# Two feed-forward up-projections in fp16 halves: weight sums move to VectorE, the norm scale moves into the norm weights, one accumulator pair takes turns over three PSUM banks

## The chip, the cores and the metric

The kernel runs on one core of one Trainium2 chip. A core has TensorE (matrix products into PSUM, eight banks of 128x512 fp32), VectorE, ScalarE and GpSimd (element-wise work, the last without PSUM), and SyncE, whose queue issues nearly all transfers between HBM and SBUF. Each engine works through its own queue in order and waits on semaphores. The metric is the device time of one execution in microseconds.

## What is computed

The reference is one layer of a transformer: half a SwiGLU feed-forward block, a token mixer with two kinds of attention, and half a SwiGLU block again, each behind an RMS norm; 1024 tokens, model width 1024, hidden width 2816. The change lies in the two feed-forward blocks:

```python
def rmsnorm(x, g):
    xf = x.astype(jnp.float32)
    y = xf * lax.rsqrt(jnp.mean(xf * xf, axis=-1, keepdims=True) + EPS)
    return (y * g.astype(jnp.float32)).astype(x.dtype)

def swiglu(h, w1, w3, w2):
    return (jax.nn.silu(h @ w1) * (h @ w3)) @ w2

h = rmsnorm(x, ffn1_norm[l])
x = x + 0.5 * swiglu(h, ffn1_w1[l], ffn1_w3[l], ffn1_w2[l])
```

All of it is fp32. TensorE multiplies in narrower formats, so the kernel splits an operand into a hi and a lo part and adds three products (hi by hi, hi by lo, lo by hi).

## The kernel before

**Work and layout.** Activations lie transposed, features on the 128 partitions (eight tiles k) and tokens along the row, in two halves tb of 512. A block runs in two stages: `ffn_up` (L309) computes silu(h w1) * (h w3) for 22 blocks of 128 hidden columns and stores them to HBM, and `ffn_down` (L522) multiplies by w2. Between the two blocks lies the token mixer, which the change does not touch.

**The up-projection.** The first four column blocks (pairs 0 and 1) are multiplied plainly in fp32 halves (L357 to L372), the accumulators being the PSUM banks X, Y and Z, two of each. Meanwhile `scale_h` (L237) forms the normed activations: x times gain times R (the reciprocal root of the mean square). `right_sums` (L274) forms four differences of them. Both leave fp16 halves by `split16` (L93): ScalarE rounds to fp16 with a scale (L94), VectorE computes what is left (L95). The scale is a power of two per norm, `K.hs`, found once in `gain_scales` (L115); its inverse is `K.hinv`.

The remaining 18 column blocks run as nine pairs fp = 2 to 10 (L412), each as one 2x2 block product with seven multiplications in place of eight (Winograd's form). The left operand has four raw blocks of 128x1024 in fp32, a11, a21, a22 and a12, loaded a pair ahead (`load`, L330). From them come four sums (L425 to L428): s1 = a21 + a22, a21 = a11 - a21, a11 = s1 - a11, s4 = a12 - a11. In pair 2 VectorE forms them, in the later pairs GpSimd (L424). `form` (L317) splits each operand into fp16 halves w: ScalarE makes hi (L94), VectorE lo (L95). The scale of a pair, a power of two, comes from the sums of squares of its raw blocks: ScalarE squares (L340), a small matmul `tot` (L344) adds over partitions, and VectorE derives `sc` and its inverse `si` (`find_scale`, L342; `pow2_scale`, L98).

TensorE's products of a pair stand, in the program's text, in this order; each is 24 matmuls of L397, twelve into each of two banks m:

| product | bank | weights, activations | read afterwards by |
|---|---|---|---|
| first product | X | a11, B11 | ScalarE, as sv (L407) |
| ws2 | Y | a11 (as a sum), T[1] | VectorE, u2 (L433) |
| ws1 | Z | s1, T[0] | |
| wa12 | X, added on | a12, B21 | ScalarE and VectorE, c11 (L442, L443) |
| ws3 | Y, added on | a21 (as a difference), T[2] | VectorE, u3 (L433, with Z L455) |
| wa22 | Y, added on | a22, T[3] | VectorE, c21 (L433) |
| ws4 | Z, added on | s4, B22 | VectorE, u2 (L469) |

Y is thus written three times in a pair and read after each; a product that is added on can start in a bank when the read before it is done, and the ws2 product of the next pair when c21 has been read. The first product of the next pair stands ahead of wa22 in the text.

Behind a product, `finish_a` (L507) applies silu on ScalarE and a product on GpSimd, and `act_sums` (L476) forms four differences on GpSimd and stores them (saT). `left_sums` (L493) loads two blocks of w2, forms four sums of them on VectorE (L503) and stores them (sw); eleven such jobs and two of `plain_sums` are spread over the pairs.

**What sets the order.** The text names dependences; a scheduler that estimates times decides the order in which each engine's instructions stand. A change of one engine's work therefore moves others too. Buffers are few: `po`, `sums` and `ex` have one of each name, so an add into u2 waits for the store of the pair before, and a w2 load for the store of the sums before.

Of the kernel before, what the change touches and what calls it, by code (L numbers as in the profile page):

```python
# [7 lines left out]
F32 = mybir.dt.float32  # L8
# [5 lines left out]
ALU = mybir.AluOpType  # L14
# [77 lines left out]

def split16(nc, t, src, scale):  # L93
    nc.scalar.activation(out=t[:, 0], in_=src, func=AF.Copy, scale=scale)  # L94
    return nc.vector.scalar_tensor_tensor(out=t[:, 1], in0=src, scalar=scale, in1=t[:, 0], op0=ALU.mult, op1=ALU.subtract)  # L95

# [18 lines left out]
def gain_scales(K, pool):  # L115
    nc = K.nc
    sq = pool.tile([P, 4, KD], F32, tag="gsq", name="gsq")
    nc.vector.tensor_tensor(out=sq, in0=K.gain, in1=K.gain, op=ALU.mult)
    r = pool.tile([P, 4], F32, tag="gr", name="gr")
    nc.vector.tensor_reduce(out=r, in_=sq, axis=AX.X, op=ALU.add)  # L120
    tot = K.pt.tile([P, TB], F32, tag="acc", name="tot")[:, 0:4]
    nc.tensor.matmul(tot, lhsT=K.ones, rhs=r, start=True, stop=True)
    K.hs, K.hinv = pow2_scale(K, pool, tot, 57)

# [112 lines left out]
def scale_h(K, tb, gi, gates=None):  # L237
    nc = K.nc
    K.h[tb], last = [None] * KD, []
    hs = K.hs[:, gi:gi + 1]  # L240
    for k in [i // 2 + i % 2 * (KD // 2) for i in range(KD)] if gates else range(KD):
        x = K.x[tb][k]
        g = K.gain[:, gi, k:k + 1]
        if gates:
            order_after(K, nc.scalar.activation(out=x, in_=x, func=AF.Copy, scale=g), gates[k])
            nc.gpsimd.tensor_tensor(out=x, in0=x, in1=K.R[tb], op=ALU.mult)
        else:
            nc.vector.scalar_tensor_tensor(out=x, in0=x, scalar=g, in1=K.R[tb], op0=ALU.mult, op1=ALU.mult)
        if gates:
            K.h[0][k] = K.hp.tile([P, 2, TB], F16, tag=f"hi0_{k}", name="h16")  # L250
            split16(nc, K.h[0][k], x, hs)
            continue
        hi = K.hp.tile([P, TB], F32R, tag=f"hi{tb}_{k}", name="hi")
        lo = K.hp.tile([P, TB], F32R, tag=f"lo{tb}_{k}", name="lo")
        last.append(split(nc, hi, lo, x))
        K.h[tb][k] = hi, lo
    if gates:
        K.b22 = []
        for k in range(KD // 2):
            K.b22.append(K.hp.tile([P, 2, TB], F16, tag=f"lo0_{k}", name="h16"))  # L260
            split16(nc, K.b22[k], K.x[1][k + KD // 2], hs)
    return last
# [10 lines left out]

def right_sums(K, tp, gi):  # L274
    nc = K.nc
    h = KD // 2
    T = [[], [], [], []]

    def put(i, k, src):
        t = (tp if i else K.hp).tile([P, 2, TB], F16, tag=f"t{i}_{k}" if i else f"lo0_{k + h}", name="tf")  # L280
        split16(nc, t, src, K.hs[:, gi:gi + 1])
        T[i].append(t)
    for k in range(h):
        b11, b21, b12, b22 = K.x[0][k], K.x[0][k + h], K.x[1][k], K.x[1][k + h]
# [24 lines left out]
def ffn_up(K, w13, w2, ctx0, gi, first):  # L309
# [7 lines left out]
    def form(src, sc):  # L317
        n = len(K.wpools)
        t = K.wpools[K.nw % n].tile([P, 2, KD, P], F16, tag=("whi", "wlo")[K.nw // n % 2], name="w16")
        K.nw += 1  # L320
        split16(nc, t.rearrange("p a k c -> p a (k c)"), src.rearrange("p k c -> p (k c)"), sc)
        return t
# [26 lines left out]
    with ExitStack() as c1:  # L349
# [7 lines left out]
        for tb, p in ((0, 0), (0, 1), (1, 1), (1, 0)):  # L357
            for f in range(2):
# [10 lines left out]
                else:  # L369
                    nc.scalar.activation(out=t, in_=u[0], func=AF.Silu)  # L370
                nc.vector.tensor_tensor(out=t, in0=u[1], in1=t, op=ALU.mult)
                store(2 * p + f, tb, t)  # L372
# [7 lines left out]
    K.nw = 0  # L380
    T = right_sums(K, open_pool(K, ctx, "tf", 1, side="right"), gi)
    ctx0.close()
    with ctx:
        pt = open_pool(K, ctx, "up_tot", 1, True)
        sums = open_pool(K, ctx, "up_sums", 1)
        rw.append(open_pool(K, ctx, "up_raw2", 1))
# [23 lines left out]
        n0, n1 = NPLAIN, NF // 2  # L410
        X, sv = first_product(r[0][0], scale, inv)
        for fp in range(n0, n1):  # L412
# [12 lines left out]
            se.tensor_tensor(out=s1, in0=a21, in1=a22, op=ALU.add)  # L425
# [1216 lines left out]
```

## Time and profile before

| | us |
|---|---|
| three runs | 2984.49, 2988.92, 2989.84; median 2988.92 |
| profiled execution | 2990.17, span 2988.4 |
| first block: plain pairs 0 and 1 / nine pairs | to 104.09 / 104.09 to 466.03 |
| first block, down-projection | from 466.03 |
| second block, nine pairs | 2403.20 to 2759.57 |
| TensorE, VectorE, ScalarE, GpSimd busy | 2835.6, 1995.5, 1370.2, 951.9 |
| mean granted TensorE clock | 0.986 of full speed |

In the views a row names line, engine, operation, output <- inputs; PE is TensorE, PEld its weight loads, DVE VectorE, ACT ScalarE, POOL GpSimd, SPq the transfer queue. A row of a timeline begins with start and length in us; what stands in brackets is the idle time of that engine in front of it and what ended it. A row of the groups ends with busy time, mean ns of one and idle time in front. Lines of code are those of the kernel before.

### The profile page before, as it was taken

To read this page: it belongs to the slowest core of one execution; us is meant where nothing else is said; L and a number is where in the kernel's file an instruction comes from. 1 tells how busy PE (TensorE), PEld (TensorE's weight loads), DVE (VectorE), ACT (ScalarE), POOL (GpSimd) and SP (SyncE) were. 2 spreads that over 40 slices of the span, in tenths; PEclk is the share of its full clock that TensorE was granted. 3 is DMA by queue.
4 is the path that set the end of the run, shared out by engine and by line. 5 is a ranking of instruction groups with operands and counts; after the bars stand their busy time and mean duration, and the time that the engine had idled before them with its cause. 6 is when DMAs were issued, how large, how long until landed. Compare 5 with 4: busy or idle time off the path is not lost. (4 is left out here: it accounts for less than half of the span.)

```text
span 2988.4 us, 40209 instructions
## 1 busy us (share of the span) xinstructions
PE 2835.6 (95%) x14276; PEld 2128.7 (71%) x14276; DVE 1995.5 (67%) x3282; ACT 1370.2 (46%) x2347; POOL 951.9 (32%) x765
## 2 busy tenths in 40 slices
PE   8998999999999899989899999999999998999998
PEld 6543447888788688778788888888878853444886
DVE  7866566666587467667777777776333966665656
ACT  7434334443333145445566666666432644432443
POOL 3348441000145123322333333333242436554101
PEclk9999999999999999999999999999999999999999
DMA  4354447655456544544332235222743246444854
GB/s 159 117 194 170 178 155 267 214 189 163 147 200 230 184 142 169 186 157 163 127 117 86 82 115 161 79 83 77 289 152 109 77 149 208 173 151 157 298 183 148
DMA packets 212712, 478.21 MB, mean 160 GB/s; under 512 B 20896, under 2 KB 39584, under 8 KB 212512
## 3 DMA queue, kind: packets, MB, share of 16 engines
q1 hardware_dynamic: 212512, 475.65, 46.2%
q8 instruction: 112, 1.84, 0.3%
q14 instruction: 88, 0.72, 0.1%
HBM read 313.56 MB, written 162.00 MB: 159 GB/s over the span
## 5 line engine op out<-in xcount | busy, mean ns | idle before, releaser
L397 PEld LDWEIGHTS <-w 128*128 128x128 f16 x3024 | 298.4, 99 | 414.4 <-issue 45.9
L52 PE MATMUL gm<-hi,whi 128*128 128x512 f32 x880 | 352.1, 400 | 3.3 <-ACT whi L89 1.9
L397 PE MATMUL Y<-tf,w 128*128 128x512 f16 x1296 | 304.2, 389 | 48.0 <-DVE u L433 29.0
L54 PE MATMUL gm<-hi,wlo 128*128 128x512 f32 x880 | 348.4, 397 | 0.3 <-DVE wlo L85 0.3
L53 PE MATMUL gm<-lo,whi 128*128 128x512 f32 x880 | 348.3, 396 | 0.0
L861 PE MATMUL S<-kt,qt 128*128 128x320 f32 (+5 forms) x1152 | 274.9, 352 | 36.4 <-ACT Pt L870 12.2
L85 DVE TENSOR_TENSOR tl<-tr,th 128x512 fp32r<-128x512 f32 (+2 forms) x384 | 236.2, 619 | 88.3 <-ACT th L89 85.0
L89 ACT ACTIVATE th<-tr 128x512 fp32r<-128x512 f32 (+2 forms) x384 | 203.8, 542 | 198.2 <-PE tr L916 194.7
L85 DVE TENSOR_TENSOR wlo<-st,whi 128x1024 fp32r<-128x1024 f32 x154 | 197.4, 1299 | 112.6 <-ACT whi L89 111.5
L868 DVE CUSTOM_DVE_ANT_0 S<-S,slab 128x896 f32<-128x896 f32 (+7 forms) x320 | 224.4, 708 | 65.5 <-PE S L861 59.5
L53 PE MATMUL acc<-wlo,whi 128*128 128x512 f32 (+1 forms) x628 | 243.1, 387 | 1.0 <-DVE wlo L85 1.0
L54 PE MATMUL acc<-whi,wlo 128*128 128x512 f32 (+1 forms) x628 | 242.1, 388 | 0.0
L89 ACT ACTIVATE whi<-st 128x1024 fp32r<-128x1024 f32 x154 | 160.6, 1057 | 177.2 <-PE acc L54 107.4
L52 PE MATMUL acc<-whi 128*128 128x512 f32 (+1 forms) x628 | 240.4, 387 | 0.0
L1027 POOL TENSOR_SCALAR Ps<-Ps,l 128x384 f32<-128x384 f32 (+7 forms) x128 | 100.8, 787 | 425.0 <-DVE l L1025 216.4
L861 PEld LDWEIGHTS S<-kt,qt 128*128 128x128 f32 x1152 | 183.4, 190 | 61.0 <-ACT Pt L870 14.2
L397 PE MATMUL X<-h,w 128*128 128x512 f16 x864 | 195.1, 379 | 0.0
L52 PEld LDWEIGHTS gm<-hi,whi 128*128 128x128 f32 x880 | 168.5, 191 | 36.3 <-ACT whi L89 2.1
L54 PEld LDWEIGHTS gm<-hi,wlo 128*128 128x128 f32 x880 | 168.1, 191 | 36.8 <-DVE wlo L85 0.9
L95 DVE SCALAR_TENSOR_TENSOR w<-a,sc,w 128x1024 f16<-128x1024 f32 x90 | 180.3, 2019 | 18.8 <-ACT w L94 17.4
L53 PEld LDWEIGHTS gm<-lo,whi 128*128 128x128 f32 x880 | 168.6, 192 | 30.8
L85 DVE TENSOR_TENSOR wlo<-wst,whi 128x1024 fp32r<-128x1024 f32 x103 | 137.0, 1332 | 44.1 <-ACT whi L89 32.9
(320 smaller groups left out, 6260.8 us busy)
## 6 DMA issues: line engine op xcount, KB each, us to landing
wst<-in_win_dram SPq DMA_DIRECT2D x55, 512.0 KB
sw<-w2s SPq DMA_DIRECT2D x44, 512.0 KB
st<-sw SPq DMA_DIRECT2D x88, 256.0 KB
st<-saT SPq DMA_DIRECT2D x88, 256.0 KB
a<-in_f1w_dram SPq DMA_DIRECT2D x36, 512.0 KB
a<-in_f2w_dram SPq DMA_DIRECT2D x36, 512.0 KB
st<-saB SPq DMA_DIRECT2D x66, 256.0 KB
qt<-sq SPq DMA_DIRECT2D x128, 128.0 KB
```

What stands on the lines that cost most here:

```text
L52: first = nc.tensor.matmul(out, lhsT=w[0][:, wk], rhs=x[0], start=start, stop=False, skip_group_check=skip)
L53: nc.tensor.matmul(out, lhsT=w[0][:, wk], rhs=x[1], start=False, stop=False, skip_group_check=skip)
L54: nc.tensor.matmul(out, lhsT=w[1][:, wk], rhs=x[0], start=False, stop=stop, skip_group_check=skip)
L85: return nc.vector.tensor_tensor(out=lo, in0=src, in1=hi.bitcast(F32), op=ALU.subtract)
L89: nc.scalar.activation(out=hi, in_=src, func=AF.Copy)
L95: return nc.vector.scalar_tensor_tensor(out=t[:, 1], in0=src, scalar=scale, in1=t[:, 0], op0=ALU.mult, op1=ALU.subtract)
L397: K.mark = nc.tensor.matmul(o, lhsT=w[:, a, m * h + k], rhs=x[k][:, b], start=start and k == 0 and i == 0, stop=k == h - 1 and i == 2, ski ...
L861: K.last = nc.tensor.matmul(S[:, o:o + n], lhsT=q, rhs=k[:, k0 + c:k0 + c + n], start=i == 0, stop=i == 1)
L868: nc.vector.tensor_tensor_reduce(out=sv, in0=sv, in1=mv, scale=-0.125, scalar=BIG, op0=ALU.add, op1=ALU.min, accum_out=nm)
L1027: nc.gpsimd.tensor_scalar(out=p[:, 0:n], in0=p[:, 0:n], scalar1=l[:, c:c + 1], scalar2=1.0, op0=ALU.mult, op1=ALU.mult)
```

## The change

Four edits. (1) The scale of the norm, `hs`, is multiplied into the norm weights once (`K.gs`); activations come out scaled, so `split16` copies and subtracts without a scale, and the plain products of the second token half are multiplied by `K.hinv` where they are read. (2) `form` keeps the weights' scale and holds the two instructions itself. (3) All weight sums are formed by VectorE. (4) Y takes two of three banks in turn, Y0, Y1 and a new Y2: pair 2 has Y0 and Y1, pair 3 has Y2 and Y0, pair 4 Y1 and Y2, and so on.

```diff
-def split16(nc, t, src, scale):
-    nc.scalar.activation(out=t[:, 0], in_=src, func=AF.Copy, scale=scale)
-    return nc.vector.scalar_tensor_tensor(out=t[:, 1], in0=src, scalar=scale, in1=t[:, 0], op0=ALU.mult, op1=ALU.subtract)
+def split16(nc, t, src):
+    nc.scalar.activation(out=t[:, 0], in_=src, func=AF.Copy)
+    return nc.vector.tensor_tensor(out=t[:, 1], in0=src, in1=t[:, 0], op=ALU.subtract)
...
-    K.hs, K.hinv = pow2_scale(K, pool, tot, 57)
+    hs, K.hinv = pow2_scale(K, pool, tot, 57)
+    K.gs = pool.tile([P, 4, KD], F32, tag="gs", name="gs")
+    nc.vector.tensor_tensor(out=K.gs, in0=K.gain, in1=hs.unsqueeze(2).broadcast_to([P, 4, KD]), op=ALU.mult)
...
-        g = K.gain[:, gi, k:k + 1]
+        g = K.gs[:, gi, k:k + 1]
...
-        split16(nc, t.rearrange("p a k c -> p a (k c)"), src.rearrange("p k c -> p (k c)"), sc)
+        hi, lo, src = [v.rearrange("p k c -> p (k c)") for v in (t[:, 0], t[:, 1], src)]
+        nc.scalar.activation(out=hi, in_=src, func=AF.Copy, scale=sc)
+        nc.vector.scalar_tensor_tensor(out=lo, in0=src, scalar=sc, in1=hi, op0=ALU.mult, op1=ALU.subtract)
...
-                    nc.scalar.activation(out=t, in_=u[0], func=AF.Silu)
-                nc.vector.tensor_tensor(out=t, in0=u[1], in1=t, op=ALU.mult)
+                    nc.scalar.activation(out=t, in_=u[0], func=AF.Silu, scale=K.hinv[:, gi:gi + 1])
+                if tb == 0:
+                    nc.vector.tensor_tensor(out=t, in0=u[1], in1=t, op=ALU.mult)
+                else:
+                    nc.vector.scalar_tensor_tensor(out=t, in0=u[1], scalar=K.hinv[:, gi:gi + 1], in1=t,
+                                                   op0=ALU.mult, op1=ALU.mult)
...
+        p3 = open_pool(K, ctx, "up_y", 1, True)
...
-            Y, Z = [[bank(n, m) for m in range(2)] for n in "YZ"]
-            se = nc.vector if fp == n0 else nc.gpsimd
+            Z = [bank("Z", m) for m in range(2)]
+            Y = [ps.tile([P, TB], F32, tag=f"Y{b}", name="Y") if b < 2 else p3.tile([P, TB], F32, tag="Y2", name="Y")
+                 for b in ((2 * (fp - n0) + m) % 3 for m in range(2))]
+            se = nc.vector
```

The scheduler's order differs from before only in the nine pairs of each block and just ahead of them; TensorE, ScalarE and SyncE issue the same instructions as before, GpSimd 64 fewer, VectorE 65 more. In the changed kernel `form`'s two halves are L323 and L324, the four sums L435 to L438, the matmuls of the pairs L405, the small matmul L347, the adds L443, L465 and L479.

VectorE at the end of pair 2, before: from the scale of pair 3 (sc_1392) to the lo half of its ws2 (w16_1524). The forms are w16, numbered one by one; c21 are the reads of Y.

```order
L106 TENSOR_SCALAR sc_1392<-sa_1391 128x1
L107 TENSOR_SCALAR sa_1391<-sa_1391 128x1
L111 TENSOR_SCALAR si_1393<-sa_1391,si_483 128x1
L433 SCALAR_TENSOR_TENSOR c21_1232<-Y_1235,si_871,s1_1201 128x512
L95 SCALAR_TENSOR_TENSOR w16_1402<-a11_1219,sc_1392,w16_1402 128x1024
L95 SCALAR_TENSOR_TENSOR w16_1527<-s1_1498,sc_1392,w16_1527 128x1024
L95 SCALAR_TENSOR_TENSOR w16_1530<-a12_1222,sc_1392,w16_1530 128x1024
L95 SCALAR_TENSOR_TENSOR w16_1533<-a21_1220,sc_1392,w16_1533 128x1024
L433 SCALAR_TENSOR_TENSOR c21_1233<-Y_1236,si_871,s1_1215 128x512
L95 SCALAR_TENSOR_TENSOR w16_1524<-a11_1219,sc_1392,w16_1524 128x1024
```

The same place on VectorE in the changed kernel; sc_1397 is the scale, w16_1529 the form of ws2, s1_1794 already a sum of pair 4.

```order
L443 SCALAR_TENSOR_TENSOR c21_1237<-Y_1242,si_873,s1_1206 128x512
L324 SCALAR_TENSOR_TENSOR w16_1407<-a11_1224,sc_1397,w16_1407 128x1024
L324 SCALAR_TENSOR_TENSOR w16_1532<-s1_1503,sc_1397,w16_1532 128x1024
L437 TENSOR_TENSOR a11_1224<-s1_1503,a11_1224 128x1024
L324 SCALAR_TENSOR_TENSOR w16_1535<-a12_1227,sc_1397,w16_1535 128x1024
L324 SCALAR_TENSOR_TENSOR w16_1538<-a21_1225,sc_1397,w16_1538 128x1024
L438 TENSOR_TENSOR s4_1504<-a12_1227,a11_1224 128x1024
L435 TENSOR_TENSOR s1_1794<-a21_1506,a22_1507 128x1024
L443 SCALAR_TENSOR_TENSOR c21_1238<-Y_1243,si_873,s1_1220 128x512
L324 SCALAR_TENSOR_TENSOR w16_1529<-a11_1224,sc_1397,w16_1529 128x1024
```

Three sums stand between the scale and ws2's lo half, among the same forms and reads. On TensorE, at the start of pair 3, the changed kernel has these rows, where before the ws2 product (Y) stood in one piece; the small matmul tot for pair 4's scale now follows four matmuls of it, and matmuls of the wa12 product (X) come in between:

```order
L405 MATMUL Y_1523<-tf_1110,w16_1529 128x512
L405 LDWEIGHTS w16_1529
L405 MATMUL Y_1524<-tf_1110,w16_1529 128x512
L405 LDWEIGHTS w16_1529
L405 MATMUL Y_1524<-tf_1110,w16_1529 128x512
L347 MATMUL tot_1683<-ss_1513,ones_297 128x4
L405 LDWEIGHTS w16_1535
L405 MATMUL X_1405<-h16_814,w16_1535 128x512
L405 LDWEIGHTS w16_1535
L405 MATMUL X_1405<-h16_814,w16_1535 128x512
```

```order
L397 MATMUL Y_1517<-tf_1152,w16_1533 128x512
L397 LDWEIGHTS w16_1533
L397 MATMUL Y_1517<-tf_1152,w16_1533 128x512
L344 MATMUL tot_1678<-ss_1508,ones_297 128x4
L397 LDWEIGHTS w16_1672
L397 MATMUL Y_1516<-tf_1112,w16_1672 128x512
```

The second piece is the end of pair 3 in the kernel before: ws3 (w16_1533), tot of pair 4, wa22 (w16_1672). In the changed kernel the first product of pair 4 stands between ws3 and wa22 there; pairs 5 and 8 have that as well, and pair 5 also the early tot. Pairs 2, 4, 6, 7 and 9 keep ws3, tot, wa22. On GpSimd, pair 3 before and after:

```order
L425 TENSOR_TENSOR s1_1789<-a21_1501,a22_1502 128x1024
L511 TENSOR_TENSOR c21_1232<-c21_1232,c21_1233 128x512
L426 TENSOR_TENSOR a21_1501<-a11_1500,a21_1501 128x1024
L511 TENSOR_TENSOR u2_1228<-u2_1228,u2_1229 128x512
L479 TENSOR_TENSOR c21_1233<-u2_1228,c11_1234 128x512
```

```order
L521 TENSOR_TENSOR c21_1237<-c21_1237,c21_1238 128x512
L521 TENSOR_TENSOR u2_1233<-u2_1233,u2_1234 128x512
L489 TENSOR_TENSOR c21_1238<-u2_1233,c11_1239 128x512
L489 TENSOR_TENSOR u2_1233<-u3_1235,u2_1233 128x512
L489 TENSOR_TENSOR u2_1234<-u3_1235,c21_1238 128x512
```

The products and differences stay in their order; the sums between them are gone.

More of the change, by code (lines that the diff above doesn't have):

```diff
@@ L239, in scale_h @@
     K.h[tb], last = [None] * KD, []
-    hs = K.hs[:, gi:gi + 1]
     for k in [i // 2 + i % 2 * (KD // 2) for i in range(KD)] if gates else range(KD):
         x = K.x[tb][k]
-        g = K.gain[:, gi, k:k + 1]
+        g = K.gs[:, gi, k:k + 1]
         if gates:
@@ L250, in scale_h @@
             K.h[0][k] = K.hp.tile([P, 2, TB], F16, tag=f"hi0_{k}", name="h16")
-            split16(nc, K.h[0][k], x, hs)
+            split16(nc, K.h[0][k], x)
             continue
@@ L260, in scale_h @@
             K.b22.append(K.hp.tile([P, 2, TB], F16, tag=f"lo0_{k}", name="h16"))
-            split16(nc, K.b22[k], K.x[1][k + KD // 2], hs)
+            split16(nc, K.b22[k], K.x[1][k + KD // 2])
     return last
@@ L271, in x_tiles, with right_sums @@
     return x
-def right_sums(K, tp, gi):
+def right_sums(K, tp):
     nc = K.nc
@@ L280, in put @@
         t = (tp if i else K.hp).tile([P, 2, TB], F16, tag=f"t{i}_{k}" if i else f"lo0_{k + h}", name="tf")
-        split16(nc, t, src, K.hs[:, gi:gi + 1])
+        split16(nc, t, src)
         T[i].append(t)
@@ L380, in ffn_up @@
     K.nw = 0
-    T = right_sums(K, open_pool(K, ctx, "tf", 1, side="right"), gi)
+    T = right_sums(K, open_pool(K, ctx, "tf", 1, side="right"))
     ctx0.close()
@@ L398, in prod, with first_product @@
                                               stop=k == h - 1 and i == 2, skip_group_check=True)
-        def first_product(a11, sc, inv):
+        def first_product(r, sc, inv):
             X = [bank("X", m) for m in range(2)]
-            w = form(a11, sc)
+            w = form(r[0][0], sc)
             s = []
@@ L410, in ffn_up @@
         n0, n1 = NPLAIN, NF // 2
-        X, sv = first_product(r[0][0], scale, inv)
+        X, sv = first_product(r, scale, inv)
         for fp in range(n0, n1):
@@ L460, in ffn_up @@
                 scale, inv = find_scale(r, pt)
-                X, nxt = first_product(r[0][0], scale, inv)
+                X, nxt = first_product(r, scale, inv)
             for m in range(2):
```

## Prediction

> **What bounds the kernel now.** I read the page first, then the windows of the two up-projection stages, then the timeline of TensorE in the first of them, then the waits of the Y banks, and last VectorE and GpSimd at the places where TensorE stood still.
>
> ```profile
> PE 2835.6 (95%) x14276; PEld 2128.7 (71%) x14276; DVE 1995.5 (67%) x3282; ACT 1370.2 (46%) x2347; POOL 951.9 (32%) x765
> 104.09:466.03 361.94, 335.44 (x1512) 149.43 (x1512) 0.98 0.48 167
> 2403.20:2759.57 356.37, 333.38 (x1512) 148.97 (x1512) 0.99 0.48 169
> 195.94 5.34 PE L397 MATMUL Z<-tf,w 128*128 128x512 f16 x24
> 201.12 5.34 PE L397 MATMUL X<-h,w 128*128 128x512 f16 x24
> ```
>
> TensorE is busy for 95% of the span, and all that the change touches lies in the stretches 104 to 466 and 2403 to 2760, where its 1512 matmuls of L397 run twice (the columns behind the stretch are its length, TensorE's time, its weight loads, granted clock, DMA share and GB/s). Undisturbed, 24 matmuls start 5.18 us after the 24 before (195.94 to 201.12). So 63 such groups need 326.3 us, and with about 1.1 us for the small matmuls of the scales 327.5. The stages take 361.94 and 356.37: they lose 34.4 and 28.9, 63.3 us together. That is all that this change can win back.
>
> The waits of the Y banks name most of it (idle us, times, over both stages), and TensorE's timeline shows where they sit:
>
> ```profile
>   DVE u L433: 29.0, 15
>   DVE w L95: 10.3, 11
>   DVE c L433: 8.7, 4
> 188.90 0.38 PE L397 MATMUL Y<-tf,w 128*128 128x512 f16 x1 [2.18 <-DVE c L433]
> 190.09 6.01 PE L397 MATMUL Y<-tf,w 128*128 128x512 f16 x21 [0.82 <-DVE w L95]
> 213.33 2.75 PE L397 MATMUL Y<-tf,w 128*128 128x512 f16 x12 [1.57 <-DVE u L433]
> 417.57 4.44 PE L397 MATMUL Y<-tf,w 128*128 128x512 f16 x12 [2.25 <-DVE u L433]
> ```
>
> There are two kinds. At a boundary between two pairs of column blocks, TensorE waits for the old Y to be read (c) and for the lo half of ws2 (w): 19.0 us. Inside a pair, between the ws3 and the wa22 product, it waits until VectorE has read Y for u3 (u): 29.0 us. The remaining 63.3 - 48.0 = 15.3 us are largely the clock: the twelve matmuls at 417.57 took 4.44 us where those at 213.33 took 2.75, so one such drop behind a wait costs 1.7 us. The waits before it were 2.2 us long.
>
> **Why VectorE is late.** Rows of VectorE and GpSimd at the boundary of pairs 2 and 3:
>
> ```profile
> 134.46 0.15 DVE L106 TENSOR_SCALAR sc<-sa 128x1 f32<-128x1 f32 x1
> 135.18 0.75 DVE L433 SCALAR_TENSOR_TENSOR c<-Y,si,s 128x512 f32<-128x512 f32 x1
> 135.85 1.27 DVE L95 SCALAR_TENSOR_TENSOR w<-a,sc,w 128x1024 f16<-128x1024 f32 x1
> 137.04 1.28 DVE L95 SCALAR_TENSOR_TENSOR w<-s,sc,w 128x1024 f16<-128x1024 f32 x1
> 138.24 6.67 DVE L95 SCALAR_TENSOR_TENSOR w<-a,sc,w 128x1024 f16<-128x1024 f32 x2
> 145.49 2.71 DVE L95 SCALAR_TENSOR_TENSOR w<-a,sc,w 128x1024 f16<-128x1024 f32 x1
> 137.26 3.28 POOL L427 TENSOR_TENSOR a<-s,a 128x1024 f32<-128x1024 f32 x1 [1.85 <-DVE w L95]
> 140.61 3.21 POOL L428 TENSOR_TENSOR s<-a,a 128x1024 f32<-128x1024 f32 x1
> 143.78 3.33 POOL L425 TENSOR_TENSOR s<-a,a 128x1024 f32<-128x1024 f32 x1
> 147.93 5.34 PE L397 MATMUL Y<-tf,w 128*128 128x512 f16 x24
> ```
>
> The same lo half of a form costs 1.27 us while GpSimd is quiet and 3.3 us (6.67 for two) or 2.71 while GpSimd forms weight sums. The rows of the first stage, by form, give the sizes (count, busy us, mean ns):
>
> ```profile
> L95 DVE SCALAR_TENSOR_TENSOR w<-a,sc,w 128x1024 f16<-128x1024 f32 x45 | 90.6, 2029 | 9.3 <-ACT w L94 8.7
> L503 DVE TENSOR_TENSOR w2s<-w2s 128x512 f32<-128x512 f32 x44 | 40.2, 913 | 38.7 <-DMA w2s<-in_f1w_dram 38.0 <-issue 0.2
> L427 DVE TENSOR_TENSOR a<-s,a 128x1024 f32<-128x1024 f32 x1 | 1.2, 1209 | 0.0
> L427 POOL TENSOR_TENSOR a<-s,a 128x1024 f32<-128x1024 f32 x8 | 22.7, 2838 | 15.0 <-DVE w L95 12.0 <-DMA saB<-u 2.9
> 104.09:466.03 361.94, 336.15 (x1529) 151.20 (x1529) 236.21 (x264) 134.77 (x180) 185.72 (x98) 0.98 0.48 167
> ```
>
> **The change, part by part.** *Sums on VectorE.* Pairs 3 to 10 move 32 sums per stage from 2.8 us on GpSimd to 1.21 us on VectorE: 39 us more on VectorE, some 92 less on GpSimd (185.72 to about 94). If the 63 forms then fall from about 2.0 to 1.28 us (45 us) and the 44 w2 sums from 0.91 to 0.69 (10 us; 0.69 is the row at 209.21 below), VectorE ends near 220 us of 327, not above its 236.21 of now. That takes away all contention; the 71 products and differences (seven in each of nine pairs, eight of the plain pairs) of 1.27 us, as in the row at 196.99 below, that stay on GpSimd can hold VectorE up by at most their own 90 us, which gives 310 of 327. VectorE still fits, but its order begins to count.
>
> The Trainium skill (SBUF — State Buffer, Who interferes with whom) says that GpSimd and a VectorE instruction with two SBUF inputs take a shared port for a whole instruction, and that the later one blocks fully; the 6.67 us above end as GpSimd's 3.28 and 3.21 us pieces end, which agrees. The adds that read PSUM (0.75 us throughout) would be free of it by the same rule.
>
> *Boundary chain.* Behind sc, the new order on VectorE has c21, two forms, the a11 sum, two forms, the s4 sum, the next pair's s1, c21 and then ws2's lo half. With 0.72 us from sc to c21, 0.67 for each c21, 1.2 per form and per sum and 1.28 for the last, that is 0.72 + 0.67 + 4.8 + 3.6 + 0.67 + 1.28 = 11.7 us, to 146.2 where now it ends at 148.20 (145.49 + 2.71). TensorE arrives 13.5 us behind sc (134.46 to 147.93) and can now first do four hi matmuls and five of X, 9 x 0.216 = 1.9 us. So no wait is left at 2 to 3 and 4 to 5. In pairs 3, 5 and 8 the scale of the next pair, or the first product, stands far earlier, so boundaries 3 to 4, 5 to 6 and 8 to 9 have half a pair to spare. At 6 to 7 and 9 to 10 the w2 sums stand in the chain and wait for their DMA: 0 to 3 us left, I take 1.0 each. The 19.0 become 2 x 2.8 = 5.6, with 0.8 of it from the first boundary of a stage, whose rows are these:
>
> ```profile
> 74.75 0.73 DVE L95 SCALAR_TENSOR_TENSOR h<-x,sc,h 128x512 f16<-128x512 f32 x1
> 54.67 0.68 DVE L85 TENSOR_TENSOR lo<-x,hi 128x512 fp32r<-128x512 f32 x1
> 108.57 6.62 DVE L95 SCALAR_TENSOR_TENSOR w<-a,sc,w 128x1024 f16<-128x1024 f32 x2
> 111.95 4.92 PE L397 MATMUL Y<-tf,w 128*128 128x512 f16 x22 [2.08 <-DVE w L95]
> 123.11 1.06 ACT L340 ACTIVATE jk<-a 128x1024 bf16<-128x1024 f32 x1
> ```
>
> A new s1 sum (1.2) stands ahead of ws2 there; against it the first of the two forms at 108.57 loses its 2.0 us of contention, and the 28 splits of activations, 0.73 us with the scale and 0.68 without, give 1.4 us. Of the 2.08, 0 to 2 stay. Gain of all boundaries 13.4, bounds 8 and 19.
>
> *A new early wait.* The scale matmul of pair 4 moves from the end of pair 3 to its start, some 148 us, and with it the sums that read pair 4's raw weights; all that TensorE does is queued behind it. It needs the squares of these weights on ScalarE, whose last began at 123.11: a margin of 24 us, and I cost it at nothing. If it went, the load of the weights (512 KB each) would show on TensorE.
>
> *Y over three banks.* It takes the c waits away (8.7 us, in the 19.0), but alone it would win little: at 188.90 the form's wait of 0.82 us follows at once, and the form ended only there. The price of the third bank is nothing: the bank is free in this stage, and no instruction is added.
>
> *Inside a pair.* The late reader is VectorE's queue, and what holds it is a transfer:
>
> ```profile
> 209.21 0.69 DVE L503 TENSOR_TENSOR w2s<-w2s 128x512 f32<-128x512 f32 x1 [4.17 <-DMA w2s<-in_f1w_dram]
> 212.53 0.74 DVE L433 SCALAR_TENSOR_TENSOR u<-Y,si,s 128x512 f32<-128x512 f32 x1
> 196.12 0.74 DVE L469 SCALAR_TENSOR_TENSOR u<-Z,si,u 128x512 f32<-128x512 f32 x1
> 191.13 3.33 POOL L426 TENSOR_TENSOR a<-a,a 128x1024 f32<-128x1024 f32 x1
> 196.99 1.27 POOL L511 TENSOR_TENSOR u<-u,u 128x512 f32<-128x512 f32 x1 [2.54 <-DMA saB<-c]
> 202.26 1.27 POOL L479 TENSOR_TENSOR u<-c,u 128x512 f32<-128x512 f32 x1
> 203.92 0.92 SPq L499 DMA_DIRECT2D w2s<-in_f1w_dram  x2
> ```
>
> The w2 load is issued at 203.92 because SP's queue holds it behind the stores of GpSimd's four differences (196.99 to 203.53), and these follow a last u2 add that VectorE made late, behind contended forms. It lands at 209.21, 5.3 us on; three more sums follow, and u3 begins at 212.53. In the new order pairs 3, 5 and 8 do the next pair's first product (24 matmuls, 5.2 us) between ws3 and wa22, which covers a wait of 1.6 to 3.2. In pairs 4, 6 and 9 the forms were made a pair earlier, so the u2 adds, the differences and the load come some 5 us sooner: no wait, at most 0.5 in all. Pair 7 keeps the old pattern behind a boundary with w2 sums in it; there ws2 ends some 3.3 us into the pair, and three forms and sums, a w2 sum and two adds later, at 8.5, the u2 adds are done. From there to the landing it is 12.3 us today (196.86 to 209.21), 11.0 with one difference less in front: 19.5. Four w2 sums, c11, three short instructions and u3 take 4.7 more, to 24.2, where TensorE arrives at 4 x 5.18 + 0.2 = 20.9: 3.3 left. With the 0.5, 2 x 3.7 = 7.4 of the 29.0 stay: gain 21.6, bounds 0 and 29.
>
> *Clock.* Where the waits of 2 us and more go, so do the drops behind them; pair 7 keeps one of 1.7 us per stage. Of the 15.3 us I count 8 as won, bounds 0 and 13.
>
> *Folded scale.* One 128x32 product, and in each stage four reads of PSUM on ScalarE and four on VectorE that now apply a scale. At most they cost what the PSUM add above costs, 0.75 us, and they replace reads that are there now; they lie in the plain products ahead of 104.09 and 2403.20, in the queue that the cheaper splits shorten. Bounds: 0 and 1 us; I take nothing.
>
> Sum: 13.4 + 21.6 + 8 = 43 us. The profiled execution took 2990.17 (span 2988.4), 1.25 above the median 2988.92 of the runs; 2990.2 - 43 = 2947, and 2946 against the median. 0.2%, 6 us, is about what a measurement of this kernel can tell from no change.
>
> **The rivals.** *The u waits stay.* If SP and the DMA engines, not GpSimd, hold the w2 load, 29.0 us and the drops behind them remain. For it: the load itself takes 5.3 us, and nothing of it changes. Against: it was issued right behind the differences. Gain 13.4 + 3: 2973.
>
> *Everything goes.* Pair 7's load is not late and no drop is left: 60 us, 2929. For it: the bounds are hand-made at 1 to 3 us. Against: VectorE's queue keeps a w2 sum before every late u3.
>
> *Slower: the sums delay ws2 in VectorE's own queue.* If GpSimd's remaining work blocks VectorE at today's rate, forms cost 2.03 and sums 1.21 x 2.03/1.28 = 1.92: the chain is 0.72 + 0.67 + 8.1 + 5.8 + 0.67 + 2.03 = 18.0 us, 152.4 instead of 148.2. Less 1.5 us of X and hi matmuls that now stand in front, four tight boundaries per stage lose 2.7 each, 21.6 us in both; the u waits stay and 8.7 of c go: 3002. It decides from the point at which ws2 ends over 15.4 us behind sc. Against: GpSimd loses half of its work.
>
> *No change: the waits move.* VectorE's in-order queue gives every boundary's win back as a u3 wait in the same pair. The Trainium skill (Perfetto Trace Analysis, Optimizing Scalar/DVE Operations) warns that shifting work between VectorE and GpSimd might not help, since they share a read port. The rows speak against it for this case, a sum being 1.21 us here and 2.84 there. 2989.
>
> **How the numbers follow.** Forecast 0.62 (its own range 2933 to 2958), u waits stay 0.22, everything goes 0.06, slower 0.06, no change 0.04. Faster by over 0.2%: 0.62 + 0.22 + 0.06 = 0.90; same 0.04; slower 0.06. The range 2930 to 2973 reaches to the first rival and leaves out about 0.15.
>
> **What would show it.** Right: forms of 128x1024 at 1.3 to 1.5 us, GpSimd near 94 us per stage, Y's idle time at about 13 us instead of 48.0, u waits only in pair 7, and both stages at 334 to 342 us. Wrong: forms still near 2 us, u L433 still near 29 us with w2 loads as late as now, or w waits at the boundaries that grew.

## The result, and the profile after

The changed kernel took 2950.62 us (median of four runs, 2947.45 to 2957.75); the kernel before took 2986.74 beside it (four runs, 2984.49 to 2989.84). The ratio is 0.9882, with a 95% interval of 0.986 to 0.9903: 1.2% faster. The prediction was 2946.0 (2930 to 2973). The profiled execution of the changed kernel is the one of 2957.75 us, 7 us above the median, so its waits are rather too large than too small.

The engines of the whole execution, and the windows of the two stages (length, TensorE, its weight loads, VectorE, ScalarE, GpSimd, granted clock, DMA share, GB/s):

```profile
PE 2830.8 (96%) x14276; PEld 2129.2 (72%) x14276; DVE 2002.1 (68%) x3347; ACT 1366.1 (46%) x2347; POOL 788.7 (27%) x701
104.16:446.34 342.18, 330.18 (x1530) 150.18 (x1529) 238.70 (x295) 133.18 (x176) 104.78 (x66) 0.99 0.51 176
2384.33:2725.93 341.60, 331.41 (x1529) 150.51 (x1529) 232.51 (x290) 128.26 (x170) 104.50 (x66) 0.99 0.50 175
```

The stages became 19.8 and 14.8 us shorter, 34.5 together; the rest of the program is 1.8 us longer (2271.9 against 2270.1). VectorE is hardly busier than before (238.70 against 236.21 us in the first stage) although it has 31 instructions more there, and GpSimd fell from 185.72 to 104.78. The groups of the first stage show why (count, busy us, mean ns):

```profile
L324 DVE SCALAR_TENSOR_TENSOR w<-a,sc,w 128x1024 f16<-128x1024 f32 x44 | 62.4, 1431 | 7.9 <-ACT w L323 7.7
L513 DVE TENSOR_TENSOR w2s<-w2s 128x512 f32<-128x512 f32 x44 | 30.2, 687 | 36.3 <-DMA w2s<-in_f1w_dram 35.8
L324 DVE SCALAR_TENSOR_TENSOR w<-s,sc,w 128x1024 f16<-128x1024 f32 x17 | 26.5, 1556 | 5.3 <-ACT w L323 5.3
L437 DVE TENSOR_TENSOR a<-s,a 128x1024 f32<-128x1024 f32 x9 | 13.9, 1548 | 0.1
L435 DVE TENSOR_TENSOR s<-a,a 128x1024 f32<-128x1024 f32 x8 | 11.7, 1468 | 0.0
```

A form fell from 2.03 to 1.43 us (from 1.77 to 1.56 where it reads s1 or s4), a w2 sum from 0.91 to 0.69; a weight sum costs about 1.5 where 1.21 had been assumed. What ended the waits of the Y banks, over both stages (us, times):

```profile
  DVE u L443: 15.6, 7
  DVE sa L105: 2.5, 2
  DVE w L324: 0.9, 2
```

The w waits are 0.9 instead of 10.3, the c waits are gone (8.7), the u waits are 15.6 instead of 29.0. The prediction worked out its chain at the boundary of pairs 2 and 3. TensorE does not wait there, and it did not before either (its row at 147.93 shows no wait). VectorE from the scale to ws2's lo half, TensorE behind it, and TensorE one pair later:

```profile
132.28 0.15 DVE L106 TENSOR_SCALAR sc<-sa 128x1 f32<-128x1 f32 x1
142.52 1.27 DVE L324 SCALAR_TENSOR_TENSOR w<-a,sc,w 128x1024 f16<-128x1024 f32 x1
145.75 1.03 PE L405 MATMUL Y<-tf,w 128*128 128x512 f16 x4
189.06 5.34 PE L405 MATMUL Z<-tf,w 128*128 128x512 f16 x24 [1.57 <-DVE u L479]
```

The lo half ends at 143.79, 11.5 us behind the scale, and TensorE arrives 13.5 us behind it: the prediction had 11.7 and 13.5. At the boundary of pairs 3 and 4, where TensorE had waited for c and w (2.18 and 0.82 us at 188.90 and 190.09), both waits are gone. But 1.57 us stand one product later (the last row), ahead of ws1, for the u2 add that reads Z; in the second stage it is 1.06.

The largest wait that is left stands in pair 5, where the prediction expected none: 5.26 us ahead of ws3 in the first stage, 3.87 in the second. The kernel before waits at the same place, 2.88 and 2.63 us. The rows of the first stage on SP, GpSimd, ScalarE, VectorE and TensorE:

```profile
212.61 8.87 POOL L489 TENSOR_TENSOR pa<-pa 128x512 f32<-128x512 f32 x4 [2.94 <-DMA pa<-saB]
214.88 4.73 SPq L490 DMA_DIRECT2D saT<-pa  x3
221.93 0.85 SPq L338 DMA_DIRECT2D a<-in_f1w_dram  x2
230.98 1.06 ACT L343 ACTIVATE jk<-a 128x1024 bf16<-128x1024 f32 x1 [5.24 <-DMA a<-in_f1w_dram]
231.35 0.15 DVE L106 TENSOR_SCALAR sc<-sa 128x1 f32<-128x1 f32 x1
233.22 1.13 ACT L323 ACTIVATE w<-a,sc 128x1024 f16<-128x1024 f32 x1
234.38 1.79 DVE L324 SCALAR_TENSOR_TENSOR w<-a,sc,w 128x1024 f16<-128x1024 f32 x1 [2.44 <-ACT w L323]
236.20 2.18 DVE L437 TENSOR_TENSOR a<-s,a 128x1024 f32<-128x1024 f32 x1
237.38 2.13 POOL L489 TENSOR_TENSOR u<-u,u 128x512 f32<-128x512 f32 x1
238.42 2.17 DVE L438 TENSOR_TENSOR s<-a,a 128x1024 f32<-128x1024 f32 x1
240.51 2.28 DVE L324 SCALAR_TENSOR_TENSOR w<-s,sc,w 128x1024 f16<-128x1024 f32 x1
242.72 0.74 DVE L443 SCALAR_TENSOR_TENSOR u<-Y,si,s 128x512 f32<-128x512 f32 x1
243.51 7.32 PE L405 MATMUL Y<-tf,w 128*128 128x512 f16 x24 [5.26 <-DVE u L443]
255.84 5.34 PE L405 MATMUL Y<-tf,w 128*128 128x512 f16 x24
```

Read from the end: ws3 waits until u2 has read Y. That read needs nothing late itself; it stands on VectorE behind two forms and two sums of pair 6. These four take 8.3 us (from 234.38 to 242.72), beside GpSimd's differences of pair 4 (the row at 237.38 is one); in a quiet place (210.11 to 213.64) such forms and sums begin 1.2 and 1.13 us apart, which gives 4.7. So 3.7 us of the wait are what the two engines take from each other.

The first of the forms also waits for its hi half, which stands on ScalarE behind two squares of pair 7's raw blocks, although pair 7's scale matmul stands at 286.92 only. The scale of pair 6 is ready at 231.50 and the hi half begins at 233.22: 1.7 us. The blocks were issued from 221.93 on, on SP behind the stores of the plain pairs' differences, for which GpSimd took 8.87 us. The two parts, estimates from these rows, make up the wait of 5.26; in the second stage they are 3.4 and 0.6 for the 3.87.

The wait also cost clock: the 24 matmuls behind it took 7.32 us, 24 others 5.34.

### The profile page after: what moved, and what is told of

The parts are those of the page before. It is cut to its first block, busy times and chain, and to the rows that moved or that the text cites. A ratio compares the mean times of both kernels' runs of the same rounds, so it can differ in the third digit from the quotient of the medians.

```text
span 2955.7 us, 40158 instructions
## 1 busy us (share of the span) xinstructions
PE 2830.8 (96%) x14276; PEld 2129.2 (72%) x14276; DVE 2002.1 (68%) x3347; ACT 1366.1 (46%) x2347; POOL 788.7 (27%) x701
## 5 line engine op out<-in xcount | busy, mean ns | idle before, releaser
L405 PEld LDWEIGHTS <-w 128*128 128x128 f16 x3024 | 297.1, 99 | 381.1 <-issue 30.4
L405 PE MATMUL Y<-tf,w 128*128 128x512 f16 x1296 | 296.7, 383 | 19.1 <-DVE u L443 15.6
L405 PE MATMUL X<-h,w 128*128 128x512 f16 x864 | 195.3, 379 | 0.5 <-ACT s L415 0.5
L85 DVE TENSOR_TENSOR wlo<-wst,whi 128x1024 fp32r<-128x1024 f32 x103 | 135.8, 1320 | 45.4 <-ACT whi L89 36.1
L1083 PE MATMUL o<-th,vt 128*128 128x256 f32 (+1 forms) x608 | 165.0, 288 | 1.6 <-ACT th L89 1.5
```

Source lines behind the costliest of these rows:

```text
L85: return nc.vector.tensor_tensor(out=lo, in0=src, in1=hi.bitcast(F32), op=ALU.subtract)
L405: K.mark = nc.tensor.matmul(o, lhsT=w[:, a, m * h + k], rhs=x[k][:, b], start=start and k == 0 and i == 0, stop=k == h - 1 and i == 2, ski ...
L1083: nc.tensor.matmul(dst, lhsT=v, rhs=hi[:, b * P:(b + n) * P], start=False, stop=False, skip_group_check=True)
```

## The experiments

All times are medians; the ratio is to the kernel before, measured beside each.

| kernel | us | ratio, 95% interval |
|---|---|---|
| changed kernel | 2950.62 | 0.9882 [0.986, 0.9903] |
| sums alone | 2945.93 | 0.9864 [0.9847, 0.9882] |
| Y over three banks alone | 2987.23 | 0.9998 [0.9989, 1.0007] |
| folded scale alone | 2987.22 | 1.0005 [0.9996, 1.0014] |
| sums and Y | 2949.32 | 0.9873 [0.9859, 0.9886] |
| changed, GpSimd kept busy | 3018.42 | 1.0104 [1.0089, 1.0119] |
| changed, GpSimd silent | 2922.92 | 0.9783 [0.9768, 0.9798] |
| changed, two buffers for u2 | 2949.35 | 0.9875 [0.9859, 0.9892] |
| changed, plain sums late | 2959.47 | 0.9907 [0.9893, 0.9922] |
| changed, differences on VectorE | 2927.85 | 0.9801 [0.9788, 0.9815] |
| changed, products on VectorE | 2939.91 | 0.9848 [0.9834, 0.9861] |
| changed, both on VectorE | 2923.58 | 0.9787 [0.9774, 0.9801] |
| both on VectorE, Y in two banks | 2923.18 | 0.9784 [0.977, 0.9797] |

### Which edit carries the gain

The first four kernels take the change apart. The theory: the sums carry it. The rival: the third Y bank or the folded scale has a share.

The sums alone, on the kernel before:

```diff
-            se = nc.vector if fp == n0 else nc.gpsimd
+            se = nc.vector
```

> The kernel before, with the weight sums of all pairs on VectorE; two Y banks and the scale in split16 as before. Theory (the sums carry the gain, by a quiet GpSimd and by the new order of products): the products stand as in the changed kernel but for two of the X matmuls at a boundary, forms fall to about 1.4 us, GpSimd to about 95 us per stage; only the waits for c21 stay, up to 8.7 us and little behind them: 2951 to 2962 us. Rival (the third Y bank carries it, the sums only fill VectorE): 2970 us or more, with c waits of 10 us and more.

2945.93 us, better than the theory's range. The c waits that the theory had left in are 1.5 us in all: with the sums off GpSimd, VectorE comes to the c21 reads in time and no third bank is needed. The rival is out.

Y over three banks alone:

```diff
+        p3 = open_pool(K, ctx, "up_y", 1, True)
...
-            Y, Z = [[bank(n, m) for m in range(2)] for n in "YZ"]
+            Z = [bank("Z", m) for m in range(2)]
+            Y = [ps.tile([P, TB], F32, tag=f"Y{b}", name="Y") if b < 2 else p3.tile([P, TB], F32, tag="Y2", name="Y")
+                 for b in ((2 * (fp - n0) + m) % 3 for m in range(2))]
```

> The kernel before, with Y over three banks and nothing else. Theory (behind each c wait stands the wait for the lo half of ws2, which does not move): the c waits of 8.7 us go, the w waits grow by nearly as much, 2982 to 2989 us, that is 0 to 5 us below the kernel before. Rival (the bank was the limit of the boundary): 8.7 us and two or three clock drops of 1.7 us each are won, 2973 to 2978 us.

2987.23 us, no difference. What ended the waits of its Y banks:

```profile
  DVE u L436: 27.1, 15
  DVE w L95: 18.7, 10
```

The c waits are gone and the w waits have grown from 10.3 to 18.7: 8.4 of the 8.7 us came back in the wait that stood behind. A wait with a second one close behind it was worth next to nothing here.

The folded scale alone (the diff is from the changed kernel: split16, the norm weights and the plain reads stay as they are there; sums on GpSimd, Y in two banks):

```diff
-            se = nc.vector
+            se = nc.vector if fp == n0 else nc.gpsimd
...
-        p3 = open_pool(K, ctx, "up_y", 1, True)
...
-            Z = [bank("Z", m) for m in range(2)]
-            Y = [ps.tile([P, TB], F32, tag=f"Y{b}", name="Y") if b < 2 else p3.tile([P, TB], F32, tag="Y2", name="Y")
-                 for b in ((2 * (fp - n0) + m) % 3 for m in range(2))]
+            Y, Z = [[bank(n, m) for m in range(2)] for n in "YZ"]
```

> The kernel before, with the norm scale folded into the norm weights and nothing else; sums on GpSimd, two Y banks. Theory (the splits lie beside TensorE's work): within 2 us of the kernel before, 2985 to 2989 us. Rival (the shorter splits of 0.68 instead of 0.73 us let the first pair start sooner): 2 to 5 us faster, all of it ahead of the nine pairs and at their first boundary.

2987.22 us: nothing that can be measured. Sums and Y without the folded scale (the kernel before, with the first two diffs of this section):

> The changed kernel without the folded scale: sums on VectorE and Y over three banks. Theory: all of the gain, within 2 us of the changed kernel, 2948 to 2953 us, with the same products order and the same two long waits for u2 in pair 5. Rival (the folded scale has a part of the gain): 2954 to 2958 us.

2949.32 us, as the theory had it, with the same long waits in pair 5 (4.19 and 3.86 us). So the sums alone are the whole gain; their time even lies below the changed kernel's, but the intervals overlap.

### Is it GpSimd's silence or the new order?

Moving the sums changed two things, GpSimd's load and the order of TensorE's products. One kernel gives GpSimd its old load back, the other takes the rest of it away.

```diff
+        idle = ex.tile([P, KD, P], F32, tag="idle", name="idle")
...
             se.tensor_tensor(out=s4, in0=a12, in1=a11, op=ALU.subtract)
+            if fp > n0:
+                for _ in range(4):
+                    nc.gpsimd.tensor_tensor(out=idle, in0=s1, in1=s1, op=ALU.add)
```

> The changed kernel, to which GpSimd adds four instructions of 128x1024 per pair from pair 3 on (s1 + s1 into a tile that nobody reads), as many and as large as the sums that were taken from it; VectorE's work and its order stay nearly the same, TensorE's products differ at the end of pair 4 only. Theory (the gain comes from a quiet GpSimd): forms go back from about 1.45 to 1.8 us and more, sums to 2 us, the products and differences stand behind the added work again; half of the gain or more goes, 2968 to 2985 us. Rival (the gain comes from the order of TensorE's products, the first product of the next pair ahead of wa22 in pairs 3, 5 and 8): 2951 to 2958 us though the forms are slow.

3018.42 us: all of the gain gone and 30 us more, beyond the theory's range. Groups of its first stage:

```profile
L442 POOL TENSOR_TENSOR idle<-s 128x1024 f32<-128x1024 f32 x32 | 80.7, 2522 | 45.5 <-DVE s L436 44.1
L324 DVE SCALAR_TENSOR_TENSOR w<-a,sc,w 128x1024 f16<-128x1024 f32 x44 | 75.0, 1715 | 8.7 <-ACT w L323 8.6
```

The window of this stage, its columns as above:

```profile
103.80:477.99 374.19, 338.08 (x1530) 151.76 (x1529) 279.69 (x295) 132.92 (x176) 186.47 (x98) 0.97 0.46 161
```

And rows of VectorE, GpSimd and TensorE in its pairs 2 and 3:

```profile
145.28 2.25 POOL L525 TENSOR_TENSOR c<-c,c 128x512 f32<-128x512 f32 x1
146.33 0.74 DVE L483 SCALAR_TENSOR_TENSOR u<-Z,si,u 128x512 f32<-128x512 f32 x1
156.31 1.89 POOL L442 TENSOR_TENSOR idle<-s 128x1024 f32<-128x1024 f32 x1
157.04 2.25 DVE L324 SCALAR_TENSOR_TENSOR w<-a,sc,w 128x1024 f16<-128x1024 f32 x1 [0.84 <-ACT w L323]
158.16 2.25 POOL L493 TENSOR_TENSOR c<-u,c 128x512 f32<-128x512 f32 x1
168.30 3.17 PE L406 MATMUL Y<-tf,w 128*128 128x512 f16 x7 [4.75 <-DVE w L324]
```

With GpSimd as busy as before the change (186.47 us), VectorE needs 279.69 us for the work that took 238.70, and TensorE waits 4.75 us for a lo half. VectorE's 128x1024 form and GpSimd's 128x512 difference, 1.27 us each when alone, both last 2.25 here: the form ends 1.1 us behind the end of GpSimd's instruction at 156.31, and the difference 1.1 us behind the end of the form. The add that reads PSUM keeps its 0.74 beside GpSimd's product at 145.28, and over all 72 u reads of Y the length is 0.73 to 0.75 us. The Trainium skill (SBUF — State Buffer, Who interferes with whom) says that a VectorE instruction with two SBUF inputs and a GpSimd instruction that reads SBUF contend, and that one with at most one SBUF input, outside the two-port modes, does not. The trace agrees.

The expectation was wrong on one thing: TensorE's products differ from pair 3's ws3 on, not at the end of pair 4 only. The added instructions also stand ahead of products and differences in GpSimd's own queue. In the trace no instruction of another engine waits for an added one. So this kernel shows that the load on GpSimd is decisive, but not how its 68 us above the changed kernel divide between the two engines' contention and GpSimd's own queue.

GpSimd silent; this kernel leaves out the products behind silu and the differences, so it does not compute the layer:

```diff
 def finish_a(K, a, b, f, tb, store):
...
-    nc.gpsimd.tensor_tensor(out=a, in0=a, in1=b, op=ALU.mult)
...
-        nc.gpsimd.tensor_tensor(out=out, in0=a, in1=b, op=ALU.subtract)
         nc.sync.dma_start(out=K.s_a[n][j], in_=out)
```

> The changed kernel without GpSimd's products behind silu and without its four differences, in the nine pairs and in the plain pairs' sums; the tiles are stored as they are, so the output lacks these steps. Theory (what is left of the waits comes from GpSimd, by the port and by the stores that u2 waits for): forms at 1.28 and sums at 1.21 us, the long u2 wait of pair 5 gone, 2925 to 2937 us. Rival (the long waits come from VectorE's order and from the stores themselves): 2942 to 2950 us.

2922.92 us, just below the range. The windows of its two stages:

```profile
104.37:431.62 327.25, 327.25 (x1529) 149.69 (x1529) 219.28 (x295) 133.51 (x176) 0.00 (x0) 1.00 0.54 185
2363.32:2690.57 327.25, 327.25 (x1529) 149.59 (x1529) 213.34 (x290) 128.54 (x170) 0.00 (x0) 1.00 0.53 184
```

Its forms, both stages together:

```profile
L324 DVE SCALAR_TENSOR_TENSOR w<-a,sc,w 128x1024 f16<-128x1024 f32 x90 | 114.2, 1278 | 16.8 <-ACT w L323 16.8
```

TensorE is busy from end to end at full clock: 327.25 us is the floor of the stage (the prediction had worked out 327.5). So the 14.9 and 14.4 us that the changed kernel still loses in its stages, 29.3 together, go when GpSimd's work goes, whether they come from contention or from what waits behind that work; VectorE's own queue, the transfers and the buffers are fast enough without it.

### The wait in pair 5

Two ideas on it, run beside those two. Two buffers for u2:

```diff
-                        u[n, m] = po.tile([P, TB], F32, tag=f"{n}{m}", name=n)
+                        u[n, m] = po.tile([P, TB], F32, tag=f"{n}{m}" + ("b" if n == "u2" and fp % 2 else ""), name=n)
```

> The changed kernel with two buffers for each u2 tile, so that the add into u2 no longer waits for the store of the pair before; VectorE's order then has u2 ahead of two forms and two sums in pair 5. Theory (pair 5's waits of 5.3 and 3.9 us for u2, and the clock drops behind them of 2 us each, come from this one buffer): both go, 2937 to 2943 us. Rival (the two sums of 2.2 us and the forms that wait for ScalarE hold u2, the store does not): waits of 2 us or more stay or move to u3, 2946 to 2951 us.

2949.35 us: the rival. VectorE reads u2 earlier and the wait ahead of ws3 is gone in both stages, but TensorE now waits at the next read in the same queue, c11, and longer than before in pair 7:

```profile
246.36 4.37 PE L405 MATMUL X<-h,w 128*128 128x512 f16 x12 [2.15 <-DVE c L453]
322.39 2.75 PE L405 MATMUL Y<-tf,w 128*128 128x512 f16 x12 [2.58 <-DVE u L443]
```

The plain pairs' sums later:

```diff
-        jobs[4:4] = [lambda p=p: plain_sums(K, ex, p) for p in range(NPLAIN)]
+        jobs[9:9] = [lambda p=p: plain_sums(K, ex, p) for p in range(NPLAIN)]
```

> The changed kernel with the sums of the plain pairs done in two of the late pairs instead of pairs 4 and 5 (w2 jobs move forward by two). Theory (these eight differences and their stores stand in front of pair 4's own, and so make u2 of pair 5 late): the waits of 5.3 and 3.9 us in pair 5 go, half of that may come back in a late pair, 2940 to 2948 us. Rival (pair 5's wait comes from VectorE's own queue): it stays at 3 us and more, 2949 to 2955 us.

2959.47 us, outside both ranges. The theory was right on the cause and wrong on the sum. Pair 5 has no such wait any more, although a form there still waits 3.19 us for a hi half behind squares; what stands behind that form is less held up. Pairs 7 and 8 wait instead, 8.4 us in the first stage (three rows below) where the changed kernel has 3.4:

```profile
318.76 2.75 PE L405 MATMUL Y<-tf,w 128*128 128x512 f16 x12 [2.26 <-DVE sa L105]
337.21 6.61 PE L405 MATMUL Y<-tf,w 128*128 128x512 f16 x22 [2.31 <-DVE w L324]
358.40 4.41 PE L405 MATMUL Y<-tf,w 128*128 128x512 f16 x12 [3.79 <-DVE u L443]
2638.41 4.44 PE L405 MATMUL Y<-tf,w 128*128 128x512 f16 x12 [5.35 <-DVE u L443]
```

The eight extra differences, with their loads and stores, make the pairs late in which they stand. Where VectorE does them the wait should go; the first and the third of the next kernels show that, in an order of their own.

### The rest of GpSimd's work on VectorE

```diff
-        nc.gpsimd.tensor_tensor(out=out, in0=a, in1=b, op=ALU.subtract)
+        nc.vector.tensor_tensor(out=out, in0=a, in1=b, op=ALU.subtract)
```

> The changed kernel with the four differences per pair (and those of the plain pairs) on VectorE instead of GpSimd: 44 instructions of 0.69 us per block, 30 us more on VectorE, 44 of 1.3 to 1.9 us less on GpSimd. Theory (what the changed kernel still loses, some 28 us, comes from GpSimd's access to SBUF beside VectorE's): half of the disturbance goes, forms at about 1.35 us, 2930 to 2943 us. Rival (VectorE's queue in order is the limit now, and more work in it makes u2 and u3 later): 2951 to 2965 us.

2927.85 us, better than the theory's range; GpSimd is busy for 40.6 us per stage, the forms take 1.31 us. The products instead:

```diff
-    nc.gpsimd.tensor_tensor(out=a, in0=a, in1=b, op=ALU.mult)
+    nc.vector.tensor_tensor(out=a, in0=a, in1=b, op=ALU.mult)
```

> The changed kernel with the three products behind silu per pair on VectorE, the differences on GpSimd. Theory (GpSimd's share): forms at about 1.38 us, 2932 to 2945 us. Rival (VectorE now waits in its queue for ScalarE's silu, and forms and adds stand behind that wait): 2951 to 2965 us.

2939.91 us, within the theory's range; GpSimd 60.8 us per stage, forms 1.35 us. Both:

> The changed kernel with the products and the differences on VectorE: 71 instructions of 0.69 us per stage, 49 us more, against about 20 us won on forms and sums; VectorE some 250 of 327 us, GpSimd idle in the nine pairs. Theory (disturbance between the two engines is the whole rest): forms at 1.28 and sums at 1.22 us, 2923 to 2938 us. Rival (order in VectorE's queue): 2945 to 2965 us though forms are at 1.28.

2923.58 us, within the theory's range, and as fast as the kernel that leaves this work out. The windows of its two stages:

```profile
103.88:432.17 328.29, 327.58 (x1530) 149.69 (x1529) 258.64 (x361) 133.27 (x176) 0.00 (x0) 1.00 0.53 184
2364.48:2691.74 327.26, 327.26 (x1530) 149.68 (x1529) 252.63 (x356) 128.72 (x170) 0.00 (x0) 1.00 0.53 183
```

Its forms and one kind of difference, both stages together, and then two rows of SP and ScalarE in pair 5:

```profile
L324 DVE SCALAR_TENSOR_TENSOR w<-a,sc,w 128x1024 f16<-128x1024 f32 x90 | 113.9, 1276 | 2.6 <-ACT w L323 2.6
L489 DVE TENSOR_TENSOR c<-u,c 128x512 f32<-128x512 f32 x18 | 12.4, 690 | 0.3
```

```profile
216.03 4.65 SPq L338 DMA_DIRECT2D a<-in_f1w_dram  x3
225.59 1.06 ACT L343 ACTIVATE jk<-a 128x1024 bf16<-128x1024 f32 x1 [6.42 <-DMA a<-in_f1w_dram]
```

VectorE took on 66 instructions in the first stage, 45.5 us at 0.69, and became only 19.9 us busier (238.70 to 258.64), since its own forms and sums were no longer held up. In pair 5 (last two rows) the raw blocks are issued some 6 us sooner than in the changed kernel and the squares begin 5.4 us sooner, 3.4 of which is TensorE's own lead there (ws2 at 218.26 against 221.62); u2's reads now stand ahead of pair 6's forms. The wait is gone, and over both stages only one of 0.7 us is left. This version leaves no step out, and it is faster than both kernels.

With Y back in two banks, the other edits as in the last kernel:

> The changed kernel with sums, products and differences all on VectorE, and Y back in two banks. Theory (with GpSimd quiet the reads of c21 come in time, so the third bank is worth nothing): within 3 us of the kernel with three banks, 2921 to 2927 us. Rival (once the forms are fast the bank is the next limit at the four boundaries per stage): waits for c of 1 us and more at each, 2929 to 2938 us.

2923.18 us, the theory: the third bank is worth nothing here either. Its waits on Y add up to 1.8 us.

## Why the prediction was right, step by step

- **All that can be won is 63.3 us.** Right. The silent kernel has 327.25 us per stage against the 327.5 worked out from one row of 5.18 us, and not a wait.
- **Forms and contention.** Right: 1.46 us over both kinds (1.43 and 1.56) against 1.3 to 1.5. GpSimd's remaining work was put at 94 us per stage and took 104.78, since it is held up as well (its share of 1.27 us per instruction became 1.6). VectorE was put at 220 us, as if no contention were left; that is the silent kernel's 219.28, the changed kernel has 238.70. One reading was loose: the two forms of 6.67 us end at 144.91, not with GpSimd's second piece (143.82) but 1.1 us behind it.
- **Boundaries: 19.0 to 5.6 us.** Better than forecast: w waits 0.9, c waits none. The chain came out at 11.5 us (11.7 forecast), at a boundary that had no wait before either. The 1.0 us each for pairs 6 to 7 and 9 to 10 did not appear, nor the 0.8 at the first boundary. But 2.6 us are new one product behind the boundary of pairs 3 and 4, where ws1 waits for the u2 add from Z; with them 3.5 are left.
- **Inside a pair: 29.0 to 7.4 us.** This term was too good by 10.7 us (and the 7.4 is a slip of 0.3 at most, since 3.3 twice and 0.5, in all or per stage, make 7.1 or 7.6): 15.6 are left, and 2.5 that the profile puts down to the small instructions of the scale (sa). The step that failed is the reading of the 29.0. The prediction put all of it between ws3 and wa22, behind the read for u3. In the trace before, half of it, 14.5 us, stands ahead of ws3, in pairs 5 and 6, where Y waits to be read for u2; the rows of the first stage:

```profile
249.42 5.34 PE L397 MATMUL Y<-tf,w 128*128 128x512 f16 x24 [2.88 <-DVE u L433]
287.37 2.75 PE L397 MATMUL Y<-tf,w 128*128 128x512 f16 x12 [1.39 <-DVE u L433]
294.21 4.37 PE L397 MATMUL Y<-tf,w 128*128 128x512 f16 x12 [3.22 <-DVE u L433]
```

  The half that the prediction did work out went as forecast in sum: the waits ahead of wa22 fell from 14.5 to 6.2 us, of which pair 7 has 1.4 and 1.1 (3.3 each forecast) and pairs 4 and 9 three of 1.1 to 1.3 (0.5 in all forecast). Pairs 3 and 8, where the first product of the next pair now stands in between, give 7.4 of the 8.3 us won. In pair 4 the w2 load was to come some 5 us sooner; it is issued 14.6 us behind the start of ws2 (196.75 against 182.15) where it was 15.0 (203.92 against 188.90), and the wait fell only from 1.57 to 1.21. The other half fell only from 14.5 to 12.0: pair 6's waits went, pair 5's grew from 5.5 to 9.1, and pair 8 has 2.9 new.
- **The early scale matmul: nothing.** Right at the matmul itself, which waits for nothing in pair 3 (146.61). But early squares of raw blocks stand in ScalarE's queue two pairs later, ahead of a hi half: 1.7 and 0.6 us of the waits in pair 5, by the rows above. The margin of 24 us was read at pair 4, where the plain pairs' sums do not stand.
- **Clock: 8 of 15.3 us.** Right in size: of the 29.3 us left, 19.0 are Y's idle time, 3.1 that of Z and X, and 7.2 the rest, so about 8 of 15.3 were won. The one drop per stage that was to stay stands in pair 5, not in pair 7.
- **Y over three banks: nothing alone.** Right, and for the reason given: the w wait behind it took 8.4 of the 8.7 us. The forecast had counted on it in the 13.4 us for boundaries; with the sums alone 7.2 of the 8.7 us of c waits go too.
- **Folded scale: nothing.** Right.
- **The sum.** 43 us forecast, 36.1 measured between the medians, 34.5 in the stages of the profiled executions. Of the 8.5 us short there (9.1 by the terms, which count 63.3 us against a floor of 327.5 and 29.3 against 327.25), 10.7 are the term inside a pair and 3.1 the waits on Z and X; boundaries gave back 4.7. So it is partly luck that the median lies only 4.6 us from the forecast.
- **The rivals.** "The u waits stay" fell as a whole, 13.4 of the 29.0 having gone, but pair 4 speaks for it: there the load came hardly sooner. "Everything goes" failed by the 19.0 us of Y waits left; its 2929 was passed only with GpSimd silent or with its differences moved. "Slower" had the right mechanism with the wrong amount of work left: with GpSimd's load put back, VectorE's queue delays its forms and the time is 3018, where the rival had said 3002. "No change" fell: forms and w2 sums became shorter, so what leaves GpSimd also gives VectorE time back. The Trainium skill (Perfetto Trace Analysis, Optimizing Scalar/DVE Operations) says that offloading operations between the two might not help because they share a read port. In this case moving them from GpSimd to VectorE helped, by 41 us for the sums alone.

What stays open: how much of the gain comes from the new order of TensorE's products by itself. The waits that ended in pairs 3 and 8, 7.4 us, are behind the new place of the first product: in pair 3 the read for u3 now ends at 170.25, 3.6 us behind the point at which ws3 gave way to that product (166.61). No kernel had the quiet GpSimd with the old order.

## What to carry to other kernels

Where VectorE and GpSimd both read SBUF all the time, price an instruction on GpSimd with what it takes from VectorE, not with its own idle time: here emptying GpSimd was worth more than balancing the two. Before counting the end of a wait as a gain, look for the next one right behind it on the same engine (8.4 of the 8.7 us of c waits came back as w waits). Before explaining a total of waits by one place, list every row in it: half of the 29.0 us stood ahead of another product than the one explained. When a step moves earlier, follow the queues of all engines that feed it at the place with the most other work, not at the first place.

## What the runs showed of the hardware that was not expected

- An instruction's length in the profile contains the time for which the other engine holds it up, on both sides: a VectorE form of 1.27 us and a GpSimd difference of 1.27 us each show 2.25 when they alternate. Work that leaves one engine also shortens what the other does: 66 instructions that take 104.78 us on GpSimd are 45.5 us on VectorE, and its busy time grows by 19.9 only.
- A load on GpSimd that no instruction of another engine waits for (32 instructions of 128x1024 per stage into an unread tile) cost 32 us in the first stage (342.18 to 374.19), although TensorE, ScalarE and VectorE had the same work. GpSimd's products and differences stand behind it, so how much of this is contention is not shown.
